# Retention and stick breaking in the third block: minus the later keys' sums in a row of each key block, one background chain for all heads, retention gated by token tile behind it

## The chip, the cores and the metric

One core of one Trainium2 chip runs the whole program. The metric is the device time of one execution in microseconds. Names of engines as in the rows below: PE is TensorE (matmul), PEld its weight load, DVE VectorE, ACT ScalarE, POOL GpSimd, SP SyncE (which issues most DMAs). All arithmetic is float32; a matmul product of two float32 matrices is made of three matmuls on a high and a low part of each (hi·hi, lo·hi, hi·lo).

## The reference

The program is a transformer of three blocks over 528 tokens (16 meta tokens, then 512) with 1024 channels. The change touches the third block, `layer_cd`, which projects the normalised tokens, mixes them in two ways, gates both, multiplies by the output weights and adds:

```python
def layer_cd(h, w_in, w_out, log_gamma, pos, valid):
    cq, ck, cv, cg, dq, dk, dv, dg = split_cols(h @ w_in, SPLIT_CD)
    oc = retention_chunked(rotary(cq), rotary(ck), cv, log_gamma)     # 4 heads
    oc = head_layer_norm(oc) * silu(cg)
    od = stick_breaking(dq, dk, dv, valid)                            # 8 heads of 64
    od = od * silu(dg)
    return concatenate([oc, od]) @ w_out

def stick_breaking(q, k, v, valid):
    z = q @ k.T * dh ** -0.5
    ok = (kpos < qpos) & valid
    log_1m = where(ok, -softplus(z), 0.0)
    after = cumsum(log_1m, axis=keys, reverse=True) - log_1m          # sum over the later keys
    w = where(ok, exp(log_sigmoid(z) + after), 0.0)
    return w @ v
```

The stick-breaking weight of a key so needs the sum of `log_1m` over all keys between it and the query. The last step of the program is an rms norm over the 512 real tokens.

## The kernel before, in words

Channels lie on partitions, tokens along the free axis: `act` is a list of eight 128-channel tiles (hi and lo). A projection of 128 output channels (`proj`, L344 on) is `f_acc` (L166 to L177): eight input tiles by three matmuls, 24 matmuls of 512 columns for the real tokens (`X`), or 24 of 272 and 24 of 256 columns for all 528 (`ALL`). Weights come by DMA on SP into `wraw` (512 KB, two buffers) and are split by ACT (`whi`, L159) and DVE (`wlo`, L160) into four buffers each. The sums land in PSUM tiles `mm` (three buffers) and are evacuated by DVE (L353, L355, L341). The chains described next use `psa` and `psb` (two buffers each) and `pso` (one).

A scheduler orders each engine's instructions by priority: program order, with `first()` raised and `chain()` raised most. Every engine then runs its list in order. Work besides the projections is written as generators in `self.bg`. `tick()` (L88) advances the first of them, and `f_acc` calls it once for three matmuls of X or six of ALL, so that a chain's matmuls stand between those of the projections. `pipe` (L1157) runs the stages of a chain in a staggered manner, with `pace` ticks between two items; `finish()` ticks until a chain is through.

Stick breaking has one generator for each pair of heads (`stick`, L1324), ten items each: key blocks 4, 3, 2, 1, 0 of 128 keys (block 4 has 16) for two heads. Blocks go from the latest keys to the earliest; block b meets the queries from its first key on, so that an item is 16, 144, 272, 400 or 512 columns wide. Stages: `logits` (two matmuls and a mask, L1342 to L1345; softplus on ACT and DVE, L1347 to L1350; its hi and lo parts, L112 and L113), `wait`, `sums` and `values` (L1390). `sums` adds to the logits, in PSUM, minus the sums within the block (`trir`, L1364) and, for blocks 3 to 0, minus the sums of the later blocks:

```python
T0, tp, tc0 = total[hh]
for part in tp:
    nc.tensor.matmul(z[:, tc0 - c0:], lhsT=self.mones[:nl, :n], rhs=part, ...)   # L1369
```

`mones` is a matrix of -1. `total` is a running elementwise sum of the softplus tiles (L1373), split again into hi and lo (`Sh`, `Sl`, L112 and L113). `exp` of the result (L1378) are the weights.

Retention is `linear` (L1223): four token tiles, stages scores (L1267, masked at L1477), attend (L1292, L1294; squares L1300, their sum L1302, 1/rms and `ot` L1306; state update L1244, L1253), norm, and finish (transposes, copied to `cqk` at L1319).

Order of `layer_cd` (L1400): projections q, k of pair 0, all of v, gate 0; pair 1 with its gate; pair 2; retention's q and k, v, gate 2; rotary and the like (L1440 to L1474, under `chain()`); then pair 3 and gate 3. `self.bg` holds stick 0, 1, 2, retention, stick 3 in that order. Then retention is finished, its four gates are projected, multiplied (L1491) and split, and its half of the output product is made (`add_out`); the rest of stick 3 runs beside these. After that `od`, the stick-breaking output, is split, and the last phase goes by token tile: transposes of the residual (L1511), the other half of the product (L1517), norm and store (L1520 to L1531).

Of the kernel before, what the change touches and what calls it, by code (L numbers as in the profile page):

```python
# [18 lines left out]
S = 512  # L19
M = 16  # L20
T = S + M
H2 = M + S // 2
D = 1024
# [37 lines left out]
class Kern:  # L61
# [265 lines left out]
    def add_out(self, mixed, toks, after=None, ws=None):  # L327
# [4 lines left out]
        for u in range(8 // per):  # L332
            w = ws[u] if ws else self.weights(nk, per * 128)
            for f in range(per):
                ps = [self.mm()[:, :t1 - t0] for t0, t1 in toks]
                self.f_acc(ps, w, f * 128, 128, mixed, toks)
# [8 lines left out]
    def proj(self, act, toks, rb, out, scale=None, nf=128):  # L345
# [4 lines left out]
        with self.first():  # L350
            for p, (t0, t1) in zip(ps, toks):
                if scale is None:
# [483 lines left out]
    def stack_q(self, p, tmp, c0):  # L836

        nc = self.nc
        a, b = (p.tile([128, T], F32R, name="qk", bufs=self.nqk) for _ in range(2))
# [14 lines left out]
    def stack_k(self, p, tmp):  # L854

        out = []
        for r in (0, 64):
            hh, ll = (p.tile([128, T], F32R, name="qk", bufs=self.nqk) for _ in range(2))
# [4 lines left out]
    def tmp(self, p):  # L863
        return p.tile([128, T], F32, name="tmp", bufs=2)
# [7 lines left out]
    def proj_k(self, p, act, rb):  # L872
        t = self.tmp(p)
        self.proj(act, ALL, rb, t)
# [12 lines left out]
    def proj_v(self, p, act, rb, tiles, outs):  # L887
# [19 lines left out]
        for f in range(4):  # L907
            t = self.tmp(p)
            self.proj(act, ALL, rb, t)
# [5 lines left out]
    def proj_va(self, p, act, out, rb):  # L915

        self.proj_v(p, act, rb, [(128 * t, min(128, T - 128 * t)) for t in range(5)], (out[:, :4], out[:M, 4]))
# [5 lines left out]
    def layer_ab(self, act, acc):  # L923
        nc, tc = self.nc, self.tc
        rb = self.norm_wide(acc, True)
        self.nqk = 12
# [231 lines left out]
    def pipe(self, stages, items, pace):  # L1158
# [3 lines left out]
        while items or on:  # L1162
            if items:
                on.append((stages, items.pop(0)))
# [6 lines left out]
            for _ in range(pace):  # L1171
# [51 lines left out]
    def linear(self, p, q, k, kx, qs, ks, v, vm, decay, att, masked, out, meta, pace):  # L1223
# [90 lines left out]
        def finish(ot, c0, n):  # L1314
# [3 lines left out]
            with self.chain():  # L1318
                nc.scalar.copy(out[:, :, c0:c0 + n], ps[:, :, :n])  # L1319
# [4 lines left out]
    def stick(self, p, cols, dv, od):  # L1324


        f, qs, ks = cols
        nc = self.nc
        om = []
        total = [None, None]  # L1330
        held = []

        def logits(hh, b):

            q = qs[hh]
            khh, kll = ks[hh]
            k0 = 128 * b
            n = min(128, T - k0)
            c0 = max(k0, M)
# [11 lines left out]
            if b < 4:  # L1351
                parts = [p.tile([128, S], F32R, name=f"L{i}", bufs=2)[:n, :w] for i in "hl"]
            else:
                parts = [p.tile([M, M], F32R, name=f"M{i}", bufs=2) for i in "hl"]
            self.split(*parts, L)
            return hh, b, n, c0, w, z, L, parts
# [4 lines left out]
        def sums(hh, b, n, c0, w, z, L, parts):  # L1361
# [3 lines left out]
            if b < 4:  # L1365
                T0, tp, tc0 = total[hh]
                nl = T0.shape[0]
                for part in tp:
                    nc.tensor.matmul(z[:, tc0 - c0:], lhsT=self.mones[:nl, :n], rhs=part, start=False, stop=True, skip_group_check=True)  # L1369
# [9 lines left out]
            return hh, b, n, c0, wt, name  # L1379

        def values(hh, b, n, c0, wt, name):
# [3 lines left out]
            if not om:  # L1385
                om.append(self.ch("o"))
# [360 lines left out]
```

## Time and profile before

| | |
|---|---|
| device time, median of 3 runs | 1196.07 us (1194.73 to 1196.13) |
| device time of the profiled execution | 1195.27 us |
| its span, first to last instruction | 1193.5 us |
| PE, DVE, ACT, POOL busy | 98%, 67%, 53%, 5% of the span |
| third block | about 902 us to the end of the span |

A row of the view by windows gives, for a stretch in microseconds from the span's start, each engine's busy time and its instructions. In the view by groups a row is a line, engine and operation, `out<-in`, partitions x elements, count; then total us, mean ns of one, and idle time before with what ended it. In the timeline a row is start and length; PE's matmuls overlap, so what one costs is read from start to start.

### The profile page before, as it was taken

The numbers are of one execution on the slowest core, as the hardware profiler recorded it, in microseconds if no ns is written. First come the engines' busy times: TensorE is split into PE (matmuls) and PEld (weight loads), VectorE is DVE, ScalarE is ACT, GpSimd is POOL, SyncE is SP. The second block draws the span as 40 slices with busy tenths as digits, with TensorE's granted clock in tenths as the row PEclk, the third lists the DMA queues.
The fourth block names the chain that finished last, engine by engine and source line by source line (L and its number), as shares of the span: only waits on it lengthen the run. The fifth ranks groups of instructions, "written<-read, shape, count | busy, mean of one in ns | idle before, by whom it ended". The sixth has DMA issues, their size and how long they took to land.

```text
span 1193.5 us, 18814 instructions
## 1 busy us (share of the span) xinstructions
PE 1172.0 (98%) x7158; PEld 1006.1 (84%) x7158; DVE 802.1 (67%) x1786; ACT 627.1 (53%) x1400; POOL 54.0 (5%) x79
## 2 busy tenths in 40 slices
PE   8999799999999999999999999999999999999997
PEld 6988688888888888888899899898999889886776
DVE  7999957544433444445799999765576486676682
ACT  6588656333322333344546345666654584566673
POOL 7000002000000000011000000000020000000000
PEclk9999999999999999999999999999999999999999
DMA  7421112323233323234322122222123223221121
GB/s 239 124 83 54 53 54 89 106 89 106 76 100 107 102 92 102 72 98 140 92 61 83 38 71 72 72 72 72 54 85 127 74 71 90 73 71 37 54 88 71
DMA packets 32907, 101.82 MB, mean 85 GB/s; under 512 B 4128, under 2 KB 4960, under 8 KB 32816
## 3 DMA queue, kind: packets, MB, share of 16 engines
q1 hardware_dynamic: 30784, 96.48, 25.3%
q0 software_dynamic: 880, 2.25, 0.7%
q10 hardware_dynamic: 1152, 1.89, 0.5%
q8 instruction: 56, 0.92, 0.3%
q14 instruction: 35, 0.29, 0.1%
HBM read 96.42 MB, written 3.10 MB: 83 GB/s over the span
## 4 chain that ended last, share of the span: by engine, by line
PE 86%; DVE 8%; ACT 3%; DMA 1%; issue 1%; DVEq 0%; SPq 0%; ACTq 0%
PE mm L174 69%; PE psb L204 4%; DVE y L708 2%; PE pso L1139 1%; DVE wlo L160 1%; PE psa L1517 1%; PE mm L1517 1%; PE pso L1390 1%; DMA x<-in_x 1%; PE pso L669 1%; PE psa L1364 1%; ACT whi L159 1%; PE psa L1101 1%; PE psb L1364 0%; PE psa L1102 0%
## 5 line engine op out<-in xcount | busy, mean ns | idle before, releaser
L174 PE MATMUL mm<-hhi,whi 128*128 128x512 f32 (+2 forms) x1280 | 433.5, 339 | 0.0
L174 PE MATMUL mm<-hhi,wlo 128*128 128x512 f32 (+2 forms) x1280 | 426.1, 333 | 2.9 <-DVE wlo L160 2.9
L174 PE MATMUL mm<-hlo,whi 128*128 128x512 f32 (+2 forms) x1280 | 426.5, 333 | 0.0
L159 ACT CAST whi<-wraw 128x512 fp32r<-128x512 f32 x346 | 205.3, 594 | 292.7 <-PE mm L174 264.3
L160 DVE TENSOR_TENSOR wlo<-wraw,whi 128x512 fp32r<-128x512 f32 x346 | 231.4, 672 | 140.3 <-ACT whi L159 118.3
L174 PEld LDWEIGHTS mm<-hhi,whi 128*128 128x128 f32 x1280 | 242.1, 189 | 24.6 <-issue 3.1
L174 PEld LDWEIGHTS mm<-hhi,wlo 128*128 128x128 f32 x1280 | 241.8, 189 | 24.8 <-DVE wlo L160 3.0
L174 PEld LDWEIGHTS mm<-hlo,whi 128*128 128x128 f32 x1280 | 242.0, 189 | 20.7
L174 PE MATMUL mm<-mx,whi 128*128 128x512 f32 (+2 forms) x448 | 113.2, 342 | 3.9 <-ACT mx L112 3.7
L174 PEld LDWEIGHTS mm<-mx,whi 128*128 128x128 f32 x448 | 76.9, 192 | 14.3 <-ACT mx L112 4.4
L813 DVE TENSOR_TENSOR gu<-mm,rb 128x512 f32<-128x512 f32 x44 | 30.4, 691 | 66.8 <-PE mm L174 66.8
L174 PE MATMUL mm<-mx,wlo 128*128 128x512 f32 (+2 forms) x224 | 74.8, 335 | 0.0
L174 PE MATMUL mm<-hidh,whi 128*128 128x512 f32 x176 | 68.5, 389 | 0.0
L174 PE MATMUL mm<-hidh,wlo 128*128 128x512 f32 x176 | 68.5, 389 | 0.0
L174 PE MATMUL mm<-hidl,whi 128*128 128x512 f32 x176 | 68.5, 389 | 0.0
L266 POOL TENSOR_TENSOR acc<-acc,sq 128x528 f32<-128x528 f32 (+1 forms) x18 | 25.6, 1421 | 774.8 <-ACT sq L264 774.8
L353 DVE TENSOR_TENSOR tmp<-mm,rb 128x272 f32<-128x272 f32 (+2 forms) x76 | 35.6, 468 | 20.3 <-PE mm L174 19.7
L174 PEld LDWEIGHTS mm<-mx,wlo 128*128 128x128 f32 x224 | 42.8, 191 | 3.6 <-issue 0.2
L708 DVE SCALAR_TENSOR_TENSOR y<-u,cols,y 128x512 f32<-128x512 f32 x60 | 42.3, 743 | 0.1
L174 PEld LDWEIGHTS mm<-hidh,whi 128*128 128x128 f32 x176 | 33.0, 188 | 6.9
L174 PEld LDWEIGHTS mm<-hidl,whi 128*128 128x128 f32 x176 | 33.0, 188 | 6.8
L174 PEld LDWEIGHTS mm<-hidh,wlo 128*128 128x128 f32 x176 | 33.0, 188 | 6.8
(452 smaller groups left out, 1790.0 us busy)
## 6 DMA issues: line engine op xcount, KB each, us to landing
wraw<-in_w SPq DMA_DIRECT2D x144, 512.0 KB, 3.5
wraw<-in_w SPq DMA_DIRECT2D x16, 384.0 KB, 3.0
wraw<-in_w SPq DMA_DIRECT2D x16, 320.0 KB, 2.7
bh<-tab SPq DMA_DIRECT2D x16, 132.0 KB, 3.0
mx<-cqk SPq DMA_DIRECT2D x8, 132.0 KB, 2.4
x<-in_x SPq DMA_DIRECT2D x4, 256.0 KB, 6.0
B<-tab POOLq DMA_DIRECT2D x4, 256.0 KB, 5.0
out<-L ACTq DMA_DIRECT2D x4, 256.0 KB, 2.5
```

What stands on the lines that cost most here:

```text
L159: self.nc.scalar.copy(hi[:, :w], raw[:, c])
L160: self.lo.tensor_tensor(out=lo[:, :w], in0=raw[:, c], in1=hi[:, :w].bitcast(F32), op=OP.subtract)
L174: nc.tensor.matmul(ps[b], lhsT=ww[i][:, f0:f0 + nf], rhs=aa[:, t0:t1], start=first and i == 0 and j == 0, stop=last and i == n - 1 and j == 2)
L204: self.nc.tensor.transpose(out, in_, self.ident[:n, :n])
L266: e.tensor_tensor(out=acc[:, c0:c1], in0=acc[:, c0:c1], in1=sq[:, c0:c1], op=OP.add)
L353: self.nc.vector.tensor_tensor(out=out[:, t0:t1], in0=p, in1=rb[:nf, t0:t1], op=OP.mult)
L669: nc.tensor.matmul(o[:, h * 64:h * 64 + 64], lhsT=pT[:, j * 128:(j + 1) * 128], rhs=vt[:, j, h * 64:h * 64 + 64], start=j == 0, stop=j == i)
L708: nc.vector.scalar_tensor_tensor(y[:, f], u[:, f, k:k + S], cw[:, f, k:k + 1], y[:, f], op0=OP.mult, op1=OP.add)
L813: nc.vector.tensor_tensor(out=t[:, g], in0=ps, in1=rbx, op=OP.mult)
L1101: nc.tensor.matmul(ps, lhsT=qs[hh][:, q0:q0 + n], rhs=khh[:, k0:k1], start=True, stop=False)
L1139: ins = nc.tensor.matmul(o[64 * e:64 * e + 64], lhsT=w, rhs=x[:, j, :n], start=i < 0 or j == 0, stop=j == 4, skip_group_check=True)
L1517: nc.tensor.matmul(ps[half], lhsT=aa[:, c], rhs=ww[:, :512], start=False, stop=k == 3 and j == 2, skip_group_check=True)
```

## The change

Key blocks are 126 keys on 128 partitions: rows 0 and 1 of each block hold no key (k and v are evacuated with two zero columns there, `gapped`). The matrix `tri` adds row 0 to every row of the block and leaves row 1 out. Row 0 of the softplus parts carries the negated value that the block before accumulated in row 0 of its own PSUM tile, that is the sum over all later keys; ACT writes its hi part (L1404), DVE its lo part (L1405), and POOL clears it for the queries that the block before did not have (L1401). The L1369 matmuls, the running total and its split are gone. Items become 24, 150, 276, 402 and 512 columns wide. One generator `sticks` runs all four pairs, with 5, 4, 4, 3 or 2 ticks an item by block, and does not begin a pair before its gate is written.

Order: pair 3 is projected before retention's v. Rotary stands right behind retention's q and k. Retention is behind the chain of all sticks, with a pace of 5. It runs during the last of the four retention gates and during the output product, which is now that of the stick-breaking channels. The first two of its products begin with three of the four input tiles (`late=3`). Retention's output is multiplied by its gate and split for each token tile (`out`), and the last phase multiplies it by the other half of the output weights, whose order in memory is swapped accordingly.

```diff
+KB = 126
+KS = KB + 2
+NB = -(-T // KB)
+TK = T + 2 * NB
@@ add_out
+            if late and u == 0:
+                for f in range(per):
+                    places.append([self.mm()[:, :t1 - t0] for t0, t1 in toks])
+                    self.f_acc(places[f], w, f * 128, 128, mixed[:late], toks, last=False)
@@ gapped: evacuation in pieces, two zero columns ahead of each block
+        def put(ps, t0, t1, rb):
+            while t0 < t1:
...
+                self.nc.vector.tensor_tensor(out=o, in0=i, in1=r, op=OP.mult)
@@ linear, finish
-                nc.scalar.copy(out[:, :, c0:c0 + n], ps[:, :, :n])
+                if callable(out):
+                    out((c0 - M) // 128, ps)
@@ sticks, logits
             self.split(*parts, L)
+            old = carry[hh]
+            new = w - old.shape[-1] if b < NB - 1 else w
+            for t in parts:
+                nc.gpsimd.memset(t[0:1, :new].bitcast(F32), 0.0)
+            if b < NB - 1:
+                hi, lo = (t[0:1, new:] for t in parts)
+                nc.scalar.mul(hi, old, -1.0)
+                nc.vector.scalar_tensor_tensor(lo, old, -1.0, hi.bitcast(F32), op0=OP.mult, op1=OP.subtract)
@@ sticks, sums
             for part in parts:
                 nc.tensor.matmul(z, lhsT=self.trir[:n, :n], rhs=part, ...)
-            if b < 4:
-                T0, tp, tc0 = total[hh]
-                for part in tp:
-                    nc.tensor.matmul(z[:, tc0 - c0:], lhsT=self.mones[:nl, :n], rhs=part, ...)
-            if b == 4:
-                total[hh] = L, parts, c0
-            elif b > 0:
-                nc.vector.tensor_tensor(out=L[:nl, tc0 - c0:], in0=L[:nl, tc0 - c0:], in1=T0, op=OP.add)
-                parts = [p.tile([128, 400], F32R, name=f"S{i}", bufs=2)[:, :w] for i in "hl"]
-                self.split(*parts, L)
-                total[hh] = L, parts, c0
+            carry[hh] = z[0:1]
@@ layer_cd
+            def out(t, ps):
+                o = p.tile([128, 4, 128], F32, name="oc")
+                for f in range(4):
+                    nc.vector.tensor_tensor(out=o[:, f], in0=ps[:, f], in1=gates[f][:, M + t * 128:M + t * 128 + 128], op=OP.mult)
+                m = self.mx()
+                hi, lo = (m[:, i, LEAD + M:].rearrange("p (f t) -> p f t", f=4) for i in range(2))
+                self.split(hi, lo, o)
+                mixed_c[t] = hi, lo
...
             for f in range(4):
-                t = self.tmp(p)
-                self.gate(p, act, X, rb, t)
-                with self.chain():
-                    nc.vector.tensor_tensor(out=cqk[:, f, M:], in0=cqk[:, f, M:], in1=t[:, M:], op=OP.mult)
-                mixed.append(self.mix(cqk[:, f, M:], M, T))
-            self.add_out(mixed, X)
-            self.finish()
-            mixed = [self.mix(od[:, f, M:], M, T) for f in range(4)]
+                gates.append(place(F32)[:, :T])
+                self.gate(p, act, X, rb, gates[f])
+            self.finish(sticks)
+            mixed = []
+            for f in range(4):
+                mixed.append([place(F32R)[:, LEAD:] for _ in range(2)])
+                with self.chain():
+                    self.split(*(t[:, M:T] for t in mixed[f]), od[:, f, M:])
+            self.add_out(mixed, X, late=3)
```

Three places in the order of the instructions. The first is PE at a `sums` stage of the first pair (`psa` holds the first head of the pair; L1364 and L1414 are the sums within a block). Before:

```order
L1390 MATMUL pso<-wt,dv 64x144 x2
L1364 MATMUL psa<-Lh,trir 128x272
L1364 MATMUL psa<-Ll,trir 128x272
L1369 MATMUL psa<-Sh,mones 128x144
L1369 MATMUL psa<-Sl,mones 128x144
L1342 MATMUL psa<-qk 128x400
L1343 MATMUL psa<-qk 128x400
```

And in the changed kernel, one block later in the keys:

```order
L1429 MATMUL pso<-wt,dv 64x24 x2
L1414 MATMUL psa<-Lh,trir 128x150
L1414 MATMUL psa<-Ll,trir 128x150
L1386 MATMUL psa<-qk 128x276
L1387 MATMUL psa<-qk 128x276
L1389 LDWEIGHTS identb
```

The two matmuls on the running total are gone from each such place, 64 in all. Over the whole program PE goes from 6864 to 6800 matmuls.

The second place is ACT in the changed kernel, where the last retention gate ends and the stick-breaking output begins to be split (`tmp_12071` is the last gate's projection, `qk_12070` that gate, L218 to L220 its sigmoid; `osq` the squares of a retention tile; L117 with `od` the hi parts of the stick-breaking output; `whi` weight casts).

```order
L164 CAST whi_12330<-wraw_12328 128x512
L1342 ACTIVATE osq_12105<-pso_12107 128x2x128
L1342 ACTIVATE osq_12105<-psb_12108 128x2x128
L237 ACTIVATE ry_12122<-rv_12120 128x4
L238 ACTIVATE ry_12122<-ry_12122 128x4
L1279 COPY kst_12143<-psb_12140 128x256
L164 CAST whi_12334<-wraw_12328 128x512
L218 ACTIVATE qk_12070<-tmp_12071 128x512
L117 CAST qk_12168<-od_9508 128x512
L219 ACTIVATE qk_12070<-qk_12070 128x512
L117 CAST qk_12172<-od_9508 128x512
```

Before, the four casts of `od` stand behind the last weight cast of the kernel, next to the last phase; now they stand behind the first step of the last gate's sigmoid, and the output product needs them.

The third place is DVE during the output product in the changed kernel (L1344 to L1348 are retention's norm, with `ot` its result; L165 weight splits; L356 the residual's addition; L1522 the gating of a token tile; L118 the lo part of that tile).

```order
L1344 TENSOR_REDUCE rs_12365<-osq_12364 128x4
L165 TENSOR_TENSOR hlo_12515<-wraw_12512,hhi_12514 128x512
L229 TENSOR_SCALAR rv_12379<-rs_12365 128x4
L165 TENSOR_TENSOR wlo_12473<-wraw_12470,whi_12472 128x512
L356 TENSOR_TENSOR x_75<-x_75,mm_12392 128x512
L242 TENSOR_TENSOR rt_12382<-ry_12381 128x4
L165 TENSOR_TENSOR wlo_12477<-wraw_12470,whi_12476 128x512
L243 SCALAR_TENSOR_TENSOR rt_12382<-rt_12382,rv_12379 128x4
L1522 TENSOR_TENSOR oc_12425<-psb_12420,qk_11891 128x128
L244 SCALAR_TENSOR_TENSOR rs_12365<-rt_12382,ry_12381 128x4
L1522 TENSOR_TENSOR oc_12425<-psb_12420,qk_11954 128x128
L1348 TENSOR_TENSOR ot_12388<-pso_12366,rs_12365 128x2x128
```

Retention's norm, the gating of the token tile before and the weight splits now share DVE's list with the output product's additions; before, this stretch had the stick-breaking softplus instead. PE transposes `ot_12388` within the product.

## Rows read from the trace of the kernel before

**Rows 1.** Windows of the third block: engines' busy us (instructions), then PEclk, DMA share, GB/s.

```profile
core 0: us, PE busy (x) PEld busy (x) DVE busy (x) ACT busy (x) POOL busy (x), PEclk, DMA share, GB/s
...
986.00:1046.00 60.00, 60.00 (x453) 53.71 (x452) 38.06 (x76) 31.22 (x74) 0.00 (x0) 1.00 0.27 80
...
1083.00:1121.00 38.00, 37.64 (x249) 26.78 (x248) 23.69 (x64) 19.40 (x51) 0.00 (x0) 1.00 0.09 29
1121.00:1156.00 35.00, 34.98 (x170) 25.17 (x169) 30.39 (x62) 30.66 (x77) 0.00 (x0) 1.00 0.33 105
...
1186.60:1193.50 6.90, 0.00 (x0) 0.00 (x0) 1.39 (x5) 1.82 (x5) 0.00 (x0) 0.84 0.20 76
```

**Rows 2.** Waits of PE, 902 to 1187 us: us in total, times, longest us.

```profile
PE psb L1364 <- ACT Lh L112: 0.3, 1, 0.3
PE psb L204 <- DVE ot L1306: 0.2, 1, 0.2
```

**Rows 3.** Timeline of PE: pairs of L1369 in four widths, to the next matmul.

```profile
955.06 0.27 PE L1369 MATMUL psa<-Mh,mones 16*128 16x16 f32 x1
...
955.37 0.39 PE L1342 MATMUL psa<-qk 128*128 128x272 f32 x1
...
1136.83 0.23 PE L1369 MATMUL psb<-Sh,mones 128*128 128x144 f32 x1
...
1137.01 0.23 PE L1345 MATMUL psa<-strict0b,identb 128*128 128x128 bf16 x1
...
1086.13 0.29 PE L1369 MATMUL psb<-Sh,mones 128*128 128x272 f32 x1
...
1086.38 0.39 PE L1364 MATMUL psa<-Lh,trir 128*128 128x512 f32 x1
...
1148.87 0.34 PE L1369 MATMUL psa<-Sh,mones 128*128 128x400 f32 x1
...
1149.23 0.39 PE L174 MATMUL mm<-mx,wlo 128*128 128x512 f32 x1
1149.46 0.40 PE L174 MATMUL mm<-mx,whi 128*128 128x512 f32 x1
```

**Rows 4.** All of L1369, 902 to 1187 us: us, PE busy (instructions), PEld, PEclk, DMA share, GB/s.

```profile
902.00:1187.00 285.00, 13.29 (x64) 10.83 (x64) 1.00 0.23 71
```

**Rows 5.** Groups of PE, third block: the widest of the value products.

```profile
L1390 PE MATMUL pso<-wt,dv 128*64 128x512 f32 x16 | 4.3, 618 | 0.1
```

**Rows 6.** Timeline of PE: one retention step, and four transposes in the last phase.

```profile
1098.68 0.38 PE L1292 MATMUL pso<-cv,att 128*128 128x128 f32 x2
...
1100.31 0.66 PE L1244 MATMUL psb<-cv,kst 128*64 128x128 f32 x8
...
1101.54 0.50 PE L174 MATMUL mm<-hlo,whi 128*128 128x512 f32 x1
...
1160.54 0.60 PE L1511 MATMUL mm<-keep,x 128*128 128x128 f32 x4
1160.89 0.48 PE L1517 MATMUL mm<-hhi,mx 128*128 128x512 f32 x1
```

**Rows 7.** Groups of DVE, ACT and (from the first block) POOL.

```profile
L160 DVE TENSOR_TENSOR wlo<-wraw,whi 128x512 fp32r<-128x512 f32 x62 | 42.8, 693 | 19.6 <-ACT whi L159 16.5 <-PE mm L174 1.1 <-PE psa L1369 1.0
...
L353 DVE TENSOR_TENSOR tmp<-mm,rb 128x256 f32<-128x256 f32 x12 | 5.1, 421 | 1.2 <-PE mm L174 1.2
...
L1302 DVE TENSOR_REDUCE rs<-osq 128x4 f32<-128x512 f32 x4 | 2.7, 686 | 5.3 <-ACT osq L1300 5.3
...
L112 ACT CAST mx<-od 128x512 fp32r<-128x512 f32 x4 | 2.5, 622 | 1.1 <-PE mm L174 0.9
...
29.57 0.12 POOL L720 MEMSET mx<- 128x4 f32 x1
```

**Rows 8.** Timeline of PE and DVE: first item of a pair, logits to their lo part.

```profile
941.05 0.17 PE L1342 MATMUL psa<-qk 128*16 128x16 f32 x1
...
944.70 0.15 DVE L113 TENSOR_TENSOR Ml<-L,Mh 16x16 fp32r<-16x16 f32 x1
```

**Rows 9.** A wait of ACT, 902 to 1187 us: us in total, times, longest us.

```profile
ACT wt L1378 <- PE psb L1369: 5.4, 5, 2.9
```

More of the change, by code (lines that the diff above doesn't have):

```diff
@@ L325, in mix, with add_out @@
         return hi, lo
-    def add_out(self, mixed, toks, after=None, ws=None):
+    def add_out(self, mixed, toks, after=None, ws=None, late=None):
         nc = self.nc
@@ L838, in stack_q @@
         nc = self.nc
-        a, b = (p.tile([128, T], F32R, name="qk", bufs=self.nqk) for _ in range(2))
+        a, b = (p.tile([128, self.wide], F32R, name="qk", bufs=self.nqk)[:, :T] for _ in range(2))
         c = slice(c0, T)
@@ L857, in stack_k @@
         for r in (0, 64):
-            hh, ll = (p.tile([128, T], F32R, name="qk", bufs=self.nqk) for _ in range(2))
+            hh, ll = (p.tile([128, self.wide], F32R, name="qk", bufs=self.nqk)[:, :tmp.shape[-1]] for _ in range(2))
             self.twice(hh, ll, tmp[r:r + 64], r)
@@ L915, in proj_va @@
     def proj_va(self, p, act, out, rb):
-        self.proj_v(p, act, rb, [(128 * t, min(128, T - 128 * t)) for t in range(5)], (out[:, :4], out[:M, 4]))
+        self.proj_v(p, act, rb, [(KS * t, min(KS, TK - KS * t)) for t in range(NB)], (out[:, :4], out[:TK - 4 * KS, 4]), True)
     def proj_vx(self, p, act, out, outm, rb):
@@ L925, in layer_ab @@
         rb = self.norm_wide(acc, True)
-        self.nqk = 12
+        self.nqk, self.wide = 12, T
         self.lo = nc.vector
@@ L1163, in pipe @@
             if items:
-                on.append((stages, items.pop(0)))
+                while ready and not ready(*items[0]):
+                    yield
+                item = items.pop(0)
+                on.append((stages, item))
             nxt = []
@@ L1170, in pipe @@
             on = nxt
-            for _ in range(pace):
+            for _ in range(pace(*item) if callable(pace) else pace):
                 yield
@@ L1318, in finish, with sticks, logits @@
             with self.chain():
-                nc.scalar.copy(out[:, :, c0:c0 + n], ps[:, :, :n])
+                if callable(out):
+                    out((c0 - M) // 128, ps)
+                else:
+                    nc.scalar.copy(out[:, :, c0:c0 + n], ps[:, :, :n])
         items = ([(-1, 0, M, vm)] if meta else []) + [(t, M + 128 * t, 128, v[:, t]) for t in range(4)]
         yield from self.pipe([scores, attend, norm, finish], items, pace)
-    def stick(self, p, cols, dv, od):
-        f, qs, ks = cols
+    def sticks(self, p, cols, dv, od):
         nc = self.nc
-        om = []
-        total = [None, None]
+        om = {}
+        carry = [None, None]
         held = []
[L1333 to L1339, printed above, removed]
+        def logits(f, hh, b):
+            q, (khh, kll) = (v[hh] for v in cols[f])
+            k0 = KS * b
+            n = min(KS, TK - k0)
+            c0 = max(KB * b, M)
             w = T - c0
@@ L1395, in values @@
                 with self.chain():
-                    nc.vector.tensor_tensor(out=od[:, f, M:], in0=om[0], in1=od[:, f, M:], op=OP.mult)
-        yield from self.pipe([logits, wait, sums, values], [(hh, b) for b in (4, 3, 2, 1, 0) for hh in range(2)], 4)
+                    nc.vector.tensor_tensor(out=od[:, f, M:], in0=om[f], in1=od[:, f, M:], op=OP.mult)
+        items = [(f, hh, b) for f in range(4) for b in reversed(range(NB)) for hh in range(2)]
+        yield from self.pipe([logits, wait, sums, values], items, lambda f, hh, b: (5, 4, 4, 3, 2)[b], lambda f, hh, b: cols[f])
     def layer_cd(self, act, acc):
@@ new lines, in layer_cd @@
+            for t in range(4):
+                vx = cv[:, t].rearrange("p (h e) -> p h e", h=4)
+                mx_ = mean[:, 4 * t:4 * t + 4]
+                nc.vector.tensor_reduce(mx_, vx, axis=AX.X, op=OP.add)
+                nc.vector.scalar_tensor_tensor(vx, mx_[:, :, None].to_broadcast([128, 4, 128]), -1.0 / 128, vx, op0=OP.mult, op1=OP.add)
+            lg = np.log(np.float32(1) - np.exp2(np.float32(-5) - np.arange(4, dtype=np.float32)))
+            dec = p.tile([128, 2], F32, name="dec")
@@ new lines, in layer_cd, with masked @@
+            for h, v in enumerate(np.exp(lg * np.float32(128))):
+                r0 = h % 2 * 64
+                nc.vector.memset(dec[r0:r0 + 64, h // 2:h // 2 + 1], float(v))
+            dmat = con("dmat").rearrange("p (h c) -> p h c", h=4)
+            def masked(a, ps, n, e):
+                nc.vector.tensor_tensor(out=a, in0=ps, in1=dmat[:n, e::2, :n], op=OP.mult)
+            gates, mixed_c = [], {}
+            def out(t, ps):
[6 more added lines that the diff above has]
+                mixed_c[t] = hi, lo
@@ L1504, in layer_cd @@
             for t in range(4):
+                while t not in mixed_c:
+                    self.tick()
+                ah, al = mixed_c[t]
                 c = slice(M + 128 * t, M + 128 * t + 128)
```

174 lines of the change are left out of this document (84 added, 90 removed).

## The prediction

> **What bounds the kernel now.** I read the windows of the third block first, then PE's waits, then the timeline at the places that the change touches. In each window of the block up to the last matmul PE is busy all the time, at the upper level of its clock (a granted clock of 1.00), while DVE is busy for 24 to 38 us of windows of 35 to 60 us, ACT for less and POOL not at all [rows 1]. PE's waits for another engine in 285 us come to 0.3 and 0.2 us [rows 2]. So the block is as long as PE's list of matmuls, plus a tail of 6.9 us without matmuls [rows 1], which the change leaves as it is. A matmul that goes away is worth its start-to-start time. A wait that is new on PE costs its whole length, because nothing else is there to take it up. Work on DVE and ACT costs nothing until PE waits for it.
>
> **Removed from PE.** The order shows 64 matmuls of L1369 gone, in 32 pairs (high and low part): eight head streams, four widths each. From the first of a pair to the next matmul the timeline shows 0.31 us at 16 columns, 0.18 at 144, 0.25 at 272 and 0.36 at 400 [rows 3]. The sum is 1.10 us, times eight 8.8 us. From above it is bounded by their 13.29 us of busy time [rows 4], which counts overlaps with the neighbours. From below: if only columns counted, the slope from 272 to 400 columns is (0.36 - 0.25) / 256 = 0.43 ns a column, and 16 x (16 + 144 + 272 + 400) columns make 5.7 us. I take 8.8, since the change removes exactly these intervals, with the turn of the array to another operand that each pair brings.
>
> A page of the Trainium skill speaks against part of this. "TensorE: Matmul & The Clock Gate", section "Wait — 56ns, not 53.3ns?", gives the start-to-start time at the upper clock as the columns divided by 2.4 GHz plus some 2.5 ns, and not below some 25 ns. By it the 64 would be worth an estimated 6.0 us and the sum below would end 2.8 us higher; the rows at 272 and 400 columns lie within 0.02 us a pair of it, those at 16 and 144 above it by 0.26 and 0.05 us.
>
> **Added to PE.** Each head stream gets 8 + 6 + 4 + 2 = 20 columns more. Four float32r matmuls a block (two logits, two sums) make 8 x 20 x 4 x 0.43 ns = 0.28 us. The value products take at most 618 / 512 = 1.2 ns a column [rows 5], so 8 x 20 x 1.2 ns = 0.19 us. Together 0.5 us.
>
> **DVE and ACT, in total.** A DVE row of w columns takes about 0.42 us + 1.06 ns x (w - 256), by the rows of 256 and 512 columns [rows 7]. By this DVE loses 24 `Sl`, 24 running totals, 8 `Ml` and 4 gate products, 21.9 us. It gains 32 carry rows (12.0), 8 lo parts of the small block (1.4), 16 gate products of 128 columns (4.6), and 8 evacuations in five pieces instead of two (3.6): 21.6 us. I price a carry row like a full tile of its width; if one partition is cheaper, this only helps. ACT loses 32 casts and 4 copies for 32 carry rows and 8 casts. So neither has more to do; what counts is where it now stands. POOL gets 96 clears, at 0.12 us each by its nearest row [rows 7]; POOL is idle here [rows 1], but the 64 matmuls of the sums that need them wait for one more engine (below).
>
> **New wait 1: last gate to output product.** Before, ACT's casts of `od` had the last gates and the output product of the retention channels ahead of them. Now the output product begins with three of these casts, and in ACT's list they stand behind the first sigmoid step of the last gate, which needs DVE's evacuation of that gate. The path is an evacuation (0.69, a 512-wide DVE row), an activation (taken as the cast beside it, 0.62) and a cast (0.62) [rows 7], 1.94 us, and DVE has two rows of 256 columns (`ot`, 0.84) that can stand ahead. PE has to cover it with an attend of one retention tile, 1098.68 to 1100.31, 1.63 us [rows 6]. 1.94 + 0.84 - 1.63 = 1.2 us, which I take; 0 if the scheduler's other matmuls fill it, 2.8 if the attend waits as well. Queued behind these ACT rows are the weight casts of the second output pair, which are not due for 24 matmuls.
>
> **New wait 2: retention beside the output product.** From the last gate's evacuation to the end of the product, DVE's list has 28 rows of 512 columns (19.4 us), 20 of 128 (5.7), 10 of 256 (4.2), 3 reductions (0.686, 2.1) [rows 7] and 12 of four columns (at 0.15 like the 16-wide row, 1.8) [rows 8]: 33.2 us. PE has 96 matmuls of 512 columns at 0.23 us [rows 3], 22.1; three retention steps of 2.86 us [rows 6], less one state update and one set of scores (1100.31 to 1101.54, 1.23), 7.35; and 16 transposes, four in 0.35 us [rows 6], 1.4. That is 30.9 us, so DVE is 2.3 us longer. Of DVE's rows the gating of the last tile (1.8) is not due until the last phase; this leaves 0.5. But DVE's list is not even: the third order shows `ot_12388`, for which PE has transposes, behind weight splits and an addition. I take 1.0 us, between 0.5 and 2.4.
>
> **New wait 3: first item of each pair.** The chain from logits to the lo part took 941.05 to 944.85, 3.8 us, with a gate's activations between its steps [rows 8]; a clear on POOL follows now. The paces put two ticks on each of these items, which gives PE 13 matmuls of 512 columns and three sets of logits for the first pair, some 3.9 us, and for the last pair, where ten of 256 columns stand, some 2.5. So 0 where the chain runs free, 1.3 where a gate stands in it. I take 0.6 for all four, ends 0 and 2.6. The clears lie in the same bounds.
>
> **Moved at no cost.** Rotary (11 DVE rows, 8 DMAs on SP) goes ahead of pair 3's projections. Before, it stood in a stretch in which DVE had 22 us free of 60 [rows 1], and PE did not wait for it [rows 2]. Its cover is now pair 3's 24 matmuls of 512 and 48 narrower ones, and three `mm` buffers; if these don't do, its price is two or three late evacuations, 2 us. On SP the DMAs pass weight loads that have two `wraw` buffers; they are short beside these, hence 0 as well. The gating of the retention channels leaves the four gates, where 4 products and 4 splits stood, and comes back within wait 2.
>
> **Sum.** 1195.27 (the profiled execution) - 8.8 + 0.5 + 1.2 + 1.0 + 0.6 = 1189.8 us. The median of the runs is 0.8 us above the profiled execution, so 1190.6 on that footing.
>
> **Rivals.**
> *No new wait.* PE finds other matmuls at all three places. For it: PE's lists before had 0.5 us of waits in all [rows 2] though chains were as dense. Against it: the output product has fewer independent matmuls than the projections before. 1195.27 - 8.8 + 0.5 + 0.8 = 1187.8. Chance 0.17.
> *The retention stretch takes the gain back.* All three waits at their upper ends, 2.8 + 2.4 + 2.6 = 7.8: 1195.6, no difference. For it: DVE is longer than PE there by the count above. Against it: PE's three accumulators and the four weight buffers even it out. Chance 0.17.
> *Slower: the carry rows block ACT and DVE.* A carry row can only start when PE has ended the sums of the block before, and both engines run in order. Before, ACT waited for these sums in `wt` 5 times for 5.4 us, 2.9 at the longest [rows 9], with no harm, since weight casts behind it had buffers. Now 32 rows more on each engine wait so, ahead of `whi` and `wlo`. If PE then starves, the change loses from (8.8 - 0.5) / 32 = 0.26 us a carry on; at 0.4 us, less than half of such a wait's mean of 1.08, it is 1195.27 - 8.3 + 12.8 + 0.8 = 1200.6. Against it: an item now has up to five ticks to the next, and the carry is due only two items later. Chance 0.11.
> *Columns only.* The removed matmuls are worth 5.7 us, and their neighbours take on the turn of the array: 1190.6 + 3.1 = 1193.7. Against it: the 16-column pair cost 0.31 us, far more than its columns [rows 3]. The page named above is this case's rule. Chance 0.06.
> That the change does not do what it says is ruled out by the order: the L1369 rows are gone.
>
> **Numbers.** My forecast has the remaining 0.49, at 1190.6 with 1187.8 to 1194 as its own range. A measurement of this kernel can tell about 0.2%, 2.4 us, from no change. Faster than 1193.7 are nearly all of the forecast (0.46), the first rival (0.17), half of the columns case (0.03) and a little of the second (0.02): 0.68. Slower than 1198.5 is most of the carry case (0.10) and a long shot of late rotary beside other waits (0.02): 0.12. The rest, 0.20, is the same. The range goes from 1185.5 (the first rival with a removed price 2.3 us nearer to its upper bound) to 1198.0, past the second rival; outside lie the carry case and a few hundredths at either end.
>
> **What would show it.** PE's busy time in the block falls by about 8 us and no L1369 row is left, else the first term is wrong. Waits of PE for `od`'s casts before the first product, for `ot` or `oc` rows of DVE within it and for the lo parts at a pair's first sums show the three waits, 1 us or so each. The carry case would show as waits of PE for `whi` or `wlo` with ACT or DVE waiting for sums at the carry rows. Columns only would show as neighbours of the sums that start as late after them as before. The forecast is wrong if PE's new waits sum to over 6 us or under 1.

## The result, and the profile after

The changed kernel takes 1186.59 us, the median of 4 runs (1184.93 to 1187.07). The kernel before took 1195.74 us beside it (4 runs, 1194.73 to 1196.13). The ratio is 0.9922, with a 95% interval from 0.9905 to 0.9939: faster by 9.2 us, where 5.5 us were forecast. The time lies in the range and below the forecast's own range; of the prediction's cases the nearest is the first rival, no new wait (1187.8 us). The profiled execution took 1186.7 us, with a span of 1184.9 us.

The page, engines' busy time:

```profile
PE 1160.0 (98%) x7094; PEld 996.0 (84%) x7094; DVE 800.0 (68%) x1806; ACT 627.0 (53%) x1404; POOL 65.3 (6%) x175
```

Before, PE was busy for 1172.0 us with 7158 matmuls. It now has 12 us less of busy time and 64 matmuls less (6864 and 6800, as counted ahead of the prediction, are not the traces' numbers; their difference is). DVE and ACT have the same as before within 2 us, and POOL has 11 us more, the clears. The windows of the third block, to set beside [rows 1] (columns as there):

```profile
940.00:1107.00 167.00, 165.62 (x1051) 134.29 (x1050) 119.34 (x245) 127.92 (x313) 11.96 (x86) 1.00 0.24 71
1107.00:1152.00 45.00, 44.93 (x273) 35.21 (x271) 35.04 (x91) 20.32 (x47) 0.00 (x0) 1.00 0.27 81
1152.00:1178.20 26.20, 26.10 (x129) 21.06 (x127) 9.20 (x26) 9.35 (x26) 0.00 (x0) 1.00 0.16 63
1178.20:1184.90 6.70, 0.00 (x0) 0.00 (x0) 1.39 (x5) 1.81 (x5) 0.00 (x0) 0.82 0.20 78
```

In the stretch where retention runs beside the output product (1107 to 1152 us) PE is still busy all the time, and DVE for 35 of 45 us. All waits of PE in the block, to set beside [rows 2]:

```profile
PE psa L1414 <- POOL Ll L1401: 0.7, 2, 0.4
PE psb L1414 <- POOL Ll L1401: 0.4, 2, 0.2
PE psb L209 <- ACT cv L935: 0.3, 1, 0.3
PE psb L304 <- ACT rbh L117: 0.2, 1, 0.2
```

**Where the time came from.** Both traces have the same landmarks on PE: the first projection matmul of the block and the last matmul of the program. Before and after:

```profile
896.67 0.40 PE L174 MATMUL mm<-hhi,whi 128*128 128x512 f32 x1
...
1186.20 0.40 PE L1517 MATMUL psa<-hlo,mx 128*128 128x512 f32 x1
```

```profile
897.45 0.40 PE L179 MATMUL mm<-hhi,whi 128*128 128x512 f32 x1
...
1177.70 0.40 PE L1566 MATMUL psa<-hlo,mx 128*128 128x512 f32 x1
```

The block went from 289.53 to 280.25 us, 9.28 us less. (The two blocks ahead of it, in which nothing was changed, ended 0.78 us later in this execution; the span so fell by 8.6 us.) The length of this block stands beside each run's time below, since the blocks ahead of it differ from one execution to another: the columns of the clock lose 5.1 us there in this profile and 10.2 in that of pace4. Summed from each matmul's start to the next one's, over the whole block, the 64 matmuls of L1369 took 8.92 us before. The logits, masks and sums within a block took 30.1 us before and 28.0 us after, 2.1 us less, although they are 20 columns wider for each head stream. The projections took 1.0 us more, with the waits for POOL among their intervals, and all else 0.75 us more.

### The profile page after: what moved, and what is told of

Its sections match the earlier page's. It is cut to its first block, busy times and chain, and to the rows that moved or that the text cites. A ratio compares the mean times of both kernels' runs of the same rounds, so it can differ in the third digit from the quotient of the medians.

```text
span 1184.9 us, 18967 instructions
## 1 busy us (share of the span) xinstructions
PE 1160.0 (98%) x7094; PEld 996.0 (84%) x7094; DVE 800.0 (68%) x1806; ACT 627.0 (53%) x1404; POOL 65.3 (6%) x175
## 3 DMA queue, kind: packets, MB, share of 16 engines
q10 hardware_dynamic: 1152, 1.89, 0.5%
## 4 chain that ended last, share of the span: by engine, by line
PE 86%; DVE 8%; ACT 3%; DMA 1%; issue 1%; POOL 0%; DVEq 0%; ACTq 0%; POOLq 0%; SPq 0%
PE mm L179 70%; PE psb L209 3%; DVE y L725 2%; DVE wlo L165 1%; PE pso L1177 1%; PE pso L1429 1%; PE psa L1566 1%; PE mm L1566 1%; PE psa L1414 1%; PE pso L686 1%; DMA x<-in_x 1%; DMA wraw<-in_w 1%; PE psb L1414 1%; ACT whi L164 1%; PE psa L1139 1%
## 5 line engine op out<-in xcount | busy, mean ns | idle before, releaser
L165 DVE TENSOR_TENSOR wlo<-wraw,whi 128x512 fp32r<-128x512 f32 x346 | 231.7, 672 | 135.8 <-ACT whi L164 116.1
L179 PE MATMUL mm<-mx,whi 128*128 128x512 f32 (+2 forms) x384 | 91.6, 331 | 5.6 <-ACT mx L117 5.5
L179 PEld LDWEIGHTS mm<-mx,whi 128*128 128x128 f32 x384 | 64.8, 192 | 11.8 <-ACT mx L117 5.9
L179 PE MATMUL mm<-mx,wlo 128*128 128x512 f32 (+2 forms) x192 | 62.1, 324 | 0.0
L370 DVE TENSOR_TENSOR tmp<-mm,rb 128x272 f32<-128x272 f32 (+2 forms) x60 | 28.9, 481 | 17.5 <-PE mm L179 16.7
L179 PEld LDWEIGHTS mm<-mx,wlo 128*128 128x128 f32 x192 | 36.6, 191 | 2.7 <-issue 0.2
```

Source lines behind the costliest of these rows:

```text
L165: self.lo.tensor_tensor(out=lo[:, :w], in0=raw[:, c], in1=hi[:, :w].bitcast(F32), op=OP.subtract)
L179: nc.tensor.matmul(ps[b], lhsT=ww[i][:, f0:f0 + nf], rhs=aa[:, t0:t1], start=first and i == 0 and j == 0, stop=last and i == n - 1 and j == 2)
```

## The experiments

The theory after this result: PE's list is the time, and the removed matmuls are all of the gain. The rival: the new order of the work has a part in it.

**1. The matmuls put back.** `zero` is a 128 x 128 matrix of zeros:

```diff
+            old = carry[hh]
+            if b < NB - 1:
+                for part in parts:
+                    nc.tensor.matmul(z[:, w - old.shape[-1]:], lhsT=zero[:n, :n], rhs=part[:, w - old.shape[-1]:], ...)
             carry[hh] = z[0:1]
```

> The changed kernel with a pair of matmuls put back at each of the 32 places: a zero matrix times columns of the softplus parts, added to the same PSUM tile, 24, 150, 276 and 402 columns wide; they add nothing to the result and wait for nothing new. Start-to-start theory (a removed pair was worth what the trace showed from its start to the next matmul, 8.8 us in all): the gain goes, about 1195.4 us, ratio to the kernel before 0.999 to 1.001. Columns only (the pairs were worth 5.7 us): about 1192.3, ratio 0.997. If the gain came from the new order and not from the matmuls: 1188 or less, ratio under 0.994.

Measured: 1193.71 us, ratio to the kernel before 0.9982 (0.9973 to 0.9991). That is 7.1 us above the changed kernel; the block took 288.16 us, 7.9 us more, and the 64 matmuls took 7.95 us from start to start. Columns only (0.997) lies just outside the interval, the start-to-start theory (0.999) just inside; the measured values lie between the two (5.7 and 8.8 us), those of the trace nearer to the second. What is missing to 8.92 us lies at the narrowest matmuls: 16 of them, on 16 partitions, took 2.50 us before, and their stand-ins, 24 columns on 128 partitions, took 1.45. The matmuls are most of the 9.2 us.

**2. The new order with the old sums.** 128-key blocks, running total and `mones`, everything else as in the changed kernel (the beginning of the edit):

```diff
-KB = 126
-KS = KB + 2
-TK = T + 2 * NB
+KB = 128
+KS = KB
+TK = T
...
```

> The new order, the single chain with its paces and the gating by token tile, but with 128-key blocks and the matmuls on the running total as before. Theory that the matmuls are all of it: ratio 0.999 to 1.002, 1194.5 to 1198 us. Rival, that the order itself gains by fewer turns of the array or fewer waits: ratio under 0.997, below 1192.5.

Measured: 1194.43 us, ratio 0.9991 (0.9983 to 1.0000), with a block of 288.79 us. The order alone gains 1 us or nothing, as the theory says. From this run to the changed kernel, with order and paces the same, the key blocks and the sums make 8.5 us of the block's 9.3.

**3. The carry rows in the old order.** The kernel before with the new `stick` stages, one generator a pair, pace 4, and `gapped`:

```diff
-            self.bg.append(self.stick(p, cols[0], dv, od))
+            self.bg.append(self.stick(p, 0, cols, dv, od))
...
```

> The kernel before with the carry rows and the gapped key blocks alone: old order, four separate chains at pace 4, retention between the third and the fourth, retention's half of the output product first. Theory that the matmuls are all of it: ratio to the kernel before 0.992 to 0.993, 1186.5 to 1187.5 us. Rival, that the carry rows need the new order and paces (in the old one ACT or DVE hold PE up at the carry rows): ratio over 0.995, with waits of PE on the sums of over 3 us.

Measured: 1197.91 us, ratio 1.0013 (1.0004 to 1.0022). The matmuls are gone and so is the gain. The rival has the time right, but not the reason: it put over 3 us of waits at the sums, and there are 1.3. The largest waits of PE in this kernel's block:

```profile
PE psb L208 <- DVE ot L1337: 2.2, 1, 2.2
PE mm L178 <- ACT mx L116: 1.2, 2, 1.0
PE mm L178 <- DVE tmp L359: 1.2, 1, 1.2
PE psa L1400 <- POOL Ll L1387: 1.0, 2, 0.5
```

With four smaller ones they come to 7.0 us. The waits for `ot` and `mx` lie at the end of retention, where the windows (columns as above) show this; the one for `tmp` comes later, from 1132.9 us on, in the output product:

```profile
1117.00:1118.00 1.00, 1.00 (x9) 0.92 (x8) 0.26 (x1) 0.96 (x3) 0.00 (x0) 1.00 0.00 0
1118.00:1119.00 1.00, 0.53 (x3) 0.09 (x1) 0.61 (x3) 0.89 (x3) 0.00 (x0) 1.00 0.00 0
1119.00:1120.00 1.00, 0.00 (x0) 0.00 (x0) 0.93 (x4) 0.26 (x2) 0.00 (x0) 1.00 0.00 0
...
1123.00:1124.00 1.00, 0.32 (x1) 0.29 (x1) 0.73 (x3) 1.00 (x3) 0.00 (x0) 0.73 0.00 0
1124.00:1125.00 1.00, 1.00 (x2) 0.50 (x2) 0.53 (x2) 1.00 (x5) 0.15 (x2) 0.50 0.00 0
...
1129.00:1130.00 1.00, 1.00 (x4) 0.81 (x3) 0.49 (x2) 1.00 (x4) 0.33 (x2) 0.50 0.00 0
1130.00:1131.00 1.00, 1.00 (x6) 0.76 (x5) 0.55 (x1) 0.41 (x1) 0.00 (x0) 0.85 0.00 0
```

PE has nothing to do for much of 5 us, and then works at a granted clock of 0.50, the 1.2 GHz level, until 1130 us. The columns of the clock lose 0.27 + 6 x 0.5 + 0.15 = 3.4 us. The whole block, in the kernel before, the changed one and this one:

```profile
896.67:1186.60 289.93, 288.92 (x1822) 238.88 (x1820) 191.68 (x401) 176.25 (x411) 0.46 (x1) 1.00 0.24 75
...
897.45:1178.10 280.65, 278.99 (x1758) 230.40 (x1756) 189.27 (x421) 176.09 (x415) 13.06 (x97) 1.00 0.26 78
...
896.72:1187.60 290.88, 283.53 (x1758) 231.93 (x1756) 188.13 (x409) 177.71 (x419) 13.13 (x97) 0.99 0.25 75
```

PE's work has shrunk here as well: it is busy for 283.5 us instead of 288.9, and 3.4 us of that are the clock's, so 8.8 us less. But it stands still for 7.4 us instead of 1.0, and that and the clock take all of it back. Against the changed kernel the block is 10.2 us longer, 5.4 us of it more waits and 3.4 us the clock. In the order of PE's instructions no projection matmul stands behind the transposes of the last `ot`; in the kernel before there are 21. The chain itself is hardly longer: from the start of the last attend matmul to that of the transposes 4.0 us, 3.6 before.

**4. The same with the new paces.**

```diff
-items, 4)
+items, lambda f, hh, b: (5, 4, 4, 3, 2)[b])
```

> Carry rows in the old order as in the run carry_old_order, with the paces of the changed kernel (5, 4, 4, 3 or 2 ticks an item by block instead of 4), still four chains. In the order of PE's instructions 12 projection matmuls then stand behind retention's last transposes, where carry_old_order has none and the kernel before has 21. Theory of cover (with the sums gone the chains reach retention's end later in PE's list, and PE runs out of projections there): the wait for ot and most of the others go, and with them the stretch at half clock; ratio to before 0.992 to 0.996, 1186.5 to 1191 us. Rival of blocked queues (ACT and DVE hold PE up at the carry rows wherever they stand): as carry_old_order, ratio 1.000 to 1.003.

Measured: 1192.28 us, ratio 0.9971 (0.9961 to 0.9982), between the two theories. The wait for `ot` is gone, a wait of 1.4 us for a retention tile's parts (`mx`) is left at that place, and the clock falls for a shorter time (1125 to 1129 us). With the paces half of the loss against the changed kernel is gone (5.6 of 11.3 us), less than was expected. No large wait is seen at the carry rows themselves (0.4 us at the sums). The block is still 5.3 us longer than the changed kernel's: more waits are 1.1 us of it (2.7 against 1.6) and the clock 1.7 us; the remaining 2.5 us were not told apart.

**5. The changed kernel with an even pace.**

```diff
-lambda f, hh, b: (5, 4, 4, 3, 2)[b], lambda
+4, lambda
```

> The changed kernel with 4 ticks an item for every block instead of 5, 4, 4, 3, 2. Theory of cover: items of the small blocks cost ticks without work, so that the single chain ends later by some 3 ticks a pair, against 9 of 168 spare; it is then drained without projections beside it and PE waits there: 1189 to 1195 us, with a stretch at half clock if the waits lie close together. Rival (the paces are for the wide blocks only and the chain has room): within 1 us of the changed kernel, 1185.6 to 1187.6.

Measured: 1189.74 us, ratio 0.9957 (0.9942 to 0.9972), 3.1 us above the changed kernel, in the range of the theory of cover; the block took 283.32 us, 3.1 us more as well. The timeline of PE and the windows at the last gate:

```profile
1110.89 0.39 PE L179 MATMUL mm<-hhi,wlo 128*128 128x512 f32 x1
1113.84 1.21 PE L179 MATMUL mm<-qk,whi 128*128 128x512 f32 x3 [2.56 <-ACT qk L117]
...
1115.41 0.63 PE L179 MATMUL mm<-qk,whi 128*128 128x512 f32 x1
1115.84 0.63 PE L179 MATMUL mm<-qk,wlo 128*128 128x512 f32 x1
```

```profile
1113.00:1114.00 1.00, 0.17 (x1) 0.17 (x2) 1.00 (x3) 1.00 (x3) 0.31 (x2) 1.00 0.17 41
1114.00:1115.00 1.00, 1.00 (x4) 0.50 (x5) 0.82 (x2) 1.00 (x3) 0.31 (x2) 0.69 0.87 291
1115.00:1116.00 1.00, 1.00 (x4) 0.81 (x4) 1.00 (x3) 1.00 (x3) 0.00 (x0) 0.50 0.48 193
1116.00:1117.00 1.00, 1.00 (x4) 0.50 (x2) 1.00 (x3) 0.63 (x2) 0.00 (x0) 0.50 0.00 0
1117.00:1118.00 1.00, 1.00 (x4) 0.59 (x3) 0.62 (x2) 0.60 (x1) 0.00 (x0) 0.61 0.46 168
```

This is the prediction's wait 1, in full: PE waits 2.56 us for the cast of `od`, and nothing stands between the last gate and the product. On ACT, casts for the last items of the stick-breaking chain (1111.61 to 1112.74 us) stand ahead of the gate's sigmoid besides. The clock that falls afterwards adds to it: a matmul of 512 columns takes 0.43 us from start to start (1115.41 to 1115.84) instead of 0.23, and the four windows lose 1.7 us. In the changed kernel the same chain runs, as the timeline of PE, DVE and ACT shows:

```profile
1117.87 0.38 PE L1334 MATMUL pso<-cv,att 128*128 128x128 f32 x2
...
1118.07 0.69 DVE L370 TENSOR_TENSOR tmp<-mm,rb 128x512 f32<-128x512 f32 x1 [0.18 <-PE mm L179]
...
1118.67 0.68 DVE L165 TENSOR_TENSOR wlo<-wraw,whi 128x512 fp32r<-128x512 f32 x1
...
1118.79 0.63 ACT L218 ACTIVATE qk<-tmp 128x512 f32<-128x512 f32 x1 [0.34 <-DVE tmp L370]
...
1119.33 0.60 ACT L117 CAST qk<-od 128x512 fp32r<-128x512 f32 x1
...
1119.98 0.50 PE L179 MATMUL mm<-qk,whi 128*128 128x512 f32 x1
```

From the evacuation to the product the chain takes 1.9 us (1118.07 to 1119.98), and PE has 2.1 us of retention (an attend and the begin of a state update, 1117.87 to 1119.98) in its list at this place. The cover is just enough: the cast ends at 1119.93 and the product begins 0.05 us later.

**6. More work for DVE beside the output product.**

```diff
+                    if late:
+                        for _ in range(1):
+                            sp = self.big.tile([128, T], F32, name="sq", tag="sq")[:, :512]
+                            nc.vector.tensor_tensor(out=sp, in0=self.x[0][:, M:T], in1=self.x[1][:, M:T], op=OP.add)
```

> The changed kernel with one more 512-wide row on DVE for each of the eight products of the stick-breaking output (an unused sum of two tiles), 5.5 us more for DVE in the stretch where retention runs beside the product. The prediction's count (DVE's list 0.5 to 2.3 us longer than PE's there): nearly all of it shows, 1190.5 to 1192.5 us. Slack (DVE was busy 35 of 45 us there and PE did not wait): within 1 us of the changed kernel, 1185.6 to 1187.6.

Measured: 1186.11 us, ratio 0.9920 (0.9907 to 0.9932), as the changed kernel (block 280.68 us). The group of the added rows, and the windows of the product and of the last phase:

```profile
L360 DVE TENSOR_TENSOR sq<-x 128x512 f32<-128x512 f32 x8 | 5.5, 685 | 0.0
```

```profile
1107.00:1152.00 45.00, 44.93 (x273) 35.39 (x273) 36.37 (x94) 17.79 (x43) 0.00 (x0) 1.00 0.15 49
1152.00:1178.00 26.00, 25.92 (x126) 20.67 (x124) 12.30 (x31) 11.41 (x29) 0.00 (x0) 1.00 0.33 120
```

DVE's stretch grew by 1.3 us only, and the last phase by 3.1 us: four of the six `hlo` splits and an addition moved out of the stretch into the last phase, where DVE had been busy for 9 of 26 us. PE waited nowhere in these two stretches. Three rows a product instead of one:

> As dve8 with three rows for each product, 16.5 us more for DVE in the stretch, where it had 10 us free. With 5.5 us nothing showed. Theory (DVE becomes the bound when its list is longer than PE's): 5 to 9 us slower than the changed kernel, 1191.5 to 1196 us, more if PE's clock falls. Rival (waits start only where a row that PE needs stands behind the added ones, and these are few): under 3 us slower.

Measured: 1187.18 us, ratio 0.9924 (0.9909 to 0.9940), with a block of 281.51 us, 1.3 us more than the changed kernel's. That is what the rival expected; the theory that DVE's list would become the bound did not come true here either, but the run loads the stretch less than was meant: 9 of the 24 rows ran in it, the others in the last phase. Where DVE becomes the bound stays open.

**7. The carry rows' load on ACT and DVE.** First, both rows written twice:

```diff
-                nc.scalar.mul(hi, old, -1.0)
-                nc.vector.scalar_tensor_tensor(lo, old, -1.0, hi.bitcast(F32), op0=OP.mult, op1=OP.subtract)
+                for _ in range(2):
+                    nc.scalar.mul(hi, old, -1.0)
+                    nc.vector.scalar_tensor_tensor(lo, old, -1.0, hi.bitcast(F32), op0=OP.mult, op1=OP.subtract)
```

> The changed kernel with each of the 32 carry rows written twice, on ACT and on DVE (the same values), some 11 us more on each engine. Theory of slack (ACT and DVE have room, items are far enough apart): within 1 us of the changed kernel, 1186 to 1187.6. Rival of blocked queues (weight casts stand behind the carry rows): a third or more of the added time reaches PE, 1190 or more.

Measured: 1197.93 us, ratio 1.0018 (1.0009 to 1.0027), 11.3 us slower than the changed kernel, with the clock at its lower level from 1078 to 1088 us. The block took 291.87 us, 11.6 us more, of which 5.6 us are more waits of PE (7.2 against 1.6) and 5.1 us the clock. This is the rival's time, but the edit adds more than load: ACT's second row has to wait until DVE has read the first, so that there are more hops between the engines, too. So with copies that nothing reads, of the same widths up to 388 columns (their tiles `spa` and `spd` are left out here):

```diff
+            if b:
+                nc.scalar.mul(spa[:, :min(w, 388)], z[0:1, :min(w, 388)], -1.0)
+                nc.vector.tensor_scalar(spd[:, :min(w, 388)], z[0:1, :min(w, 388)], -1.0, None, op0=OP.mult)
```

> The changed kernel with an unused copy of each of the 32 carry rows on ACT and on DVE (388 columns at most, into a tile of one row that nothing reads): engine time as in carry_twice, but no new step in a chain. In this kernel's order only a set of scores stands between the last gate and the output product, as in clear_dve, so 1 to 2 us of wait are expected there in any case. Theory of latency (carry_twice lost 11 us since its second pair of rows waits on the first across engines, twice): 1187 to 1190 us. Theory of blocked queues (32 rows of ACT and DVE are enough): 1192 us or more, with waits of PE at sums or weights all along the chain.

Measured: 1191.36 us, ratio 0.9958 (0.9944 to 0.9971), between the two theories; the block took 284.71 us, 4.5 us more than the changed kernel's. The largest waits of PE:

```profile
PE mm L179 <- ACT qk L117: 1.3, 1, 1.3
PE psb L1416 <- ACT Lh L1406: 1.0, 2, 0.7
PE psa L1416 <- POOL Ll L1403: 0.8, 2, 0.6
PE psb L1416 <- ACT L L1394: 0.6, 1, 0.6
```

All together 5.3 us: 1.6 us for `od` (`qk`) at the last gate, as was expected, and 3.3 us at the sums, where the changed kernel has 1.1. Some 11 us of extra work on each engine so cost PE 2.2 us more along the chain, 0.07 us a carry: the changed kernel has cover for most of such work, but not for all. The block of carry_twice is another 7.2 us longer: 5.1 us the clock and 1.9 us more waits, to which the hops belong.

**8. The clears on POOL, and the first cast.** Row 0 cleared once on DVE, ahead of the split:

```diff
+            nc.vector.memset(L[0:1, :new], 0.0)
             self.split(*parts, L)
-            for t in parts:
-                nc.gpsimd.memset(t[0:1, :new].bitcast(F32), 0.0)
```

> The changed kernel with row 0's new columns cleared once on DVE ahead of the split, instead of twice on POOL behind it: POOL's waits (1.1 us on PE in the changed kernel) go, DVE gets 40 short rows. If PE's waits for POOL are latency alone: 1185.0 to 1186.0. If DVE's own rows take their place: 1186.6 to 1188.

Measured: 1187.20 us, ratio 0.9932 (0.9920 to 0.9944), no clear difference to the changed kernel (block 280.99 us, 0.7 us more). The time is in the second range, but not because of DVE's rows, for which PE does not wait. POOL's waits are gone; instead the scheduler left only a set of scores at the last gate, and wait 1 came back:

```profile
PE mm L179 <- ACT qk L117: 1.7, 1, 1.7
```

After this wait the clock stayed at 1.00. Then, on top, with the parts of `od`'s first tile made ahead of the last gate (`od_parts(f)` is the split of tile f):

```diff
             for f in range(4):
+                if f == 3:
+                    od_parts(0)
                 gates.append(place(F32)[:, :T])
...
```

> clear_dve (row 0 cleared on DVE ahead of the split) with the first stick-breaking tile's parts made ahead of the last gate instead of behind it. In its order nothing stands between the last gate and the output product. Theory (the wait of 1.7 us in clear_dve is the path gate, sigmoid, cast): the first product starts at once, then waits for the second tile's parts for about 1 us at most; 1185.2 to 1187 us. Rival (the list of ACT, not the first cast, sets it): as clear_dve or slower, 1187 to 1189.

Measured: 1186.38 us, ratio 0.9915 (0.9901 to 0.9929). The wait for `od` is gone (1.0 us of other waits are left), and the time is that of the changed kernel within the interval (block 280.33 us).

**9. Without `late`.**

```diff
-self.add_out(mixed, X, late=3)
+self.add_out(mixed, X)
```

> The changed kernel without late: each product of the output takes its four input tiles at once, so that the fourth tile's parts are due 9 matmuls after the first product begins. In the changed kernel the fourth cast ended at 1123.06 us, 3.1 us after the product began (1119.98), with state updates and scores of retention among the matmuls. If these cover it: 1186 to 1187.2 us. If late was needed: a wait of 0.5 to 1.5 us on the fourth parts, 1187.2 to 1189.

Measured: 1185.99 us, ratio 0.9916 (0.9902 to 0.9930), with a block of 280.08 us and no wait of PE between 1107 us and the end. `late` was not needed in this order. No run is clearly faster than the changed kernel.

## Why the prediction came out as it did

Direction and range were right, by the main term; the gain was 3.7 us larger than forecast. The steps that failed were "New wait 1" and "New wait 2", 2.2 us of waits that did not come, and the term for added columns. In the block the added columns came out 2.5 us better than forecast and the waits 1.7 us (1.1 us more than before instead of 2.8), all else 0.5 us worse. The new waits are just above the 1 us under which the prediction called itself wrong.

- **Removed from PE, 8.8 us.** Right: 8.9 us in the trace, and 7.1 us (time) or 7.95 us (trace) when as many matmuls were put back. Columns alone do not price so short matmuls: the slope of the wider ones made 5.7 us of them. By "TensorE: Matmul & The Clock Gate" of the Trainium skill, section "Wait — 56ns, not 53.3ns?", they are worth an estimated 6.0 us; the measurements of this case are above it.
- **Added to PE, 0.5 us.** Wrong in sign: the logits, masks and sums got 2.1 us shorter from start to start, in spite of their columns. The order is not the reason: in order_only they take 30.0 us, as before. In sums_back, with the new key blocks and the matmuls put back, they take 28.5, so that 1.5 us come with the new blocks; the largest piece is the 16 sums of 144 columns, 2.71 us, which became 1.73 us with 150. Why these are faster stays open.
- **New wait 1, 1.2 us: none came.** The path was sized well (1.9 us). The cover was not: 2.1 us of retention instead of 1.63, and the two rows of `ot` that were laid ahead of the path had already run. That the mechanism is real, and hangs on what the scheduler lays between gate and product, pace4 (2.6 us) and clear_dve (1.7 us) show; that it costs nothing in the changed kernel, by 0.05 us, is luck.
- **New wait 2, 1.0 us: none came.** DVE's rows were counted rightly, but their lengths do not add up. From the last gate's evacuation to the end of the product the changed kernel shows this (columns as above):

```profile
1118.07:1152.00 33.93, 33.88 (x194) 26.75 (x193) 28.25 (x73) 15.21 (x35) 0.00 (x0) 1.00 0.29 85
```

DVE has 73 rows, as counted, and their lengths make 33.1 us, against 33.2 in the prediction; but it is busy for 28.3, since a row can begin before the one ahead of it has ended (1118.67 against 1118.07 + 0.69 in the timeline above). PE takes 33.9 us instead of 30.9. So DVE's list is 5.7 us shorter than PE's where the prediction had it 2.3 us longer. Due dates give it more room: the weight splits for the last phase are not due before it, and dve8 pushed four of them there.
- **New wait 3, 0.6 us: 1.1 us came**, three of its four pieces at a pair's first item, and all of them on POOL's clears, which were put "in the same bounds".
- **Moved at no cost.** Right for rotary: PE waits nowhere in pair 3's projections.
- **The rival of blocked queues** was given a price of 12.8 us and 0.11. The runs bear out a small part of it: 32 rows more cost PE 2.2 us at the sums. What the prediction did not see is what decides: in the old order the same change loses the whole gain, most of it for want of matmuls beside the end of retention. The order and the paces, which without the new sums are worth 1 us or nothing, are what lets PE keep the 9 us: the paces give back half of the loss, and how the order gives back the rest is shown in part only (experiment 4). They were costed as waits that they add, and not as waits that they prevent.

## What to carry to other kernels

Matmuls that leave a bound PE also leave the latency chains beside them without cover: before and after such a change, look at the one place where a chain ends and no independent matmul is left, and lay an independent product there. A wait on PE at such a place costs more than its length if the clock falls after it. Work that can be done later is no load on a stretch: count a list by due dates, not by its sum, and price its rows from start to start, on DVE as on PE.

## What the runs showed of the hardware that was not expected

Waits of a few microseconds can cost the clock as well. In pace4 PE stood still for 2.56 us and then worked at 0.50 until about 1117.6 us, which took 1.7 us on top. In carry_old_order it was busy for 2.3 of the 6 us from 1118 to 1124 and at 0.50 for some 6.8 us from there, 3.4 us on top. In carry_old_pace a wait of 1.37 us, with shorter ones before it, was followed by a lower clock from 1125 to 1129 us, 1.7 us on top. In clear_dve PE stood still for 1.70 us and the clock did not fall. So the length of a single wait does not tell by itself whether the clock falls.
